# Sublayer boundaries of a conditioned trunk: three engines in written order, four weight blocks converted ahead, conditioning loads two tiles ahead

## The chip, the cores and the metric

The kernel runs on one core of one Trainium2 chip. The metric is the device time of one execution in microseconds; the kernel before was timed three times, with a median of 1191.43 us (1189.97 to 1196.67). On the core, TensorE (PE) multiplies, VectorE (DVE) and ScalarE (ACT) do the elementwise work, SyncE (SP) issues nearly all loads, and GpSimd (POOL) issues a few small ones.

## The reference, cut to what matters

Two layers, each of three sublayers: a SwiGLU feed-forward, a token mixer (HGRN2 gated recurrence in layer 0, chunked gMLP in layer 1) and another feed-forward. The input is 256 tokens of 1024 features in float32.

```python
def sublayer(x, fn, pre_g, post_g, shift, scale, gate, res_w):
    h = rms_norm(x, pre_g) * (1.0 + scale) + shift
    return x + res_w * gate * rms_norm(fn(h), post_g)

def swiglu(h, w_in, w_out):
    a, b = jnp.split(h @ w_in, 2, axis=-1)
    return (jax.nn.silu(a) * b) @ w_out
...
    cond = jax.nn.silu(c)
    for i in range(DEPTH):
        mod = (cond @ ada_w[i] + ada_b[i]).reshape(B, 3 * N_SUB, D_MODEL)[:, :, None, :]
```

`shift`, `scale` and `gate` of every sublayer are rows of `mod`, the conditioning product of a 1024-vector with a large matrix.

## The kernel before

**Split numbers.** Every float32 operand of a large product is held as two parts of TensorE's reduced float32 type: a high part (a cast) and a low part (what the cast left over). A product is three matmuls: high with high, high with low, low with high (`mm3`, lines 140 to 144; `mm3f`, 332 to 336; `chunk2`, 322 to 330, joins two of them).

**Weights.** They come in 188 blocks of 128 x 2048, in the order of use. `wblock` (112 to 125) brings one as two halves: a 512 KB load into one of four `raw` buffers, the cast by ScalarE (line 119), the subtraction by VectorE (line 120). The parts lie in tiles of the pool `whl`, twelve of them, six blocks. `next_block` converts until `ahead` blocks are in hand beyond the one it gives out. Block 33 is the first of the HGRN sublayer, 53, 86, 119 and 155 are the first of the next four.

**Conditioning.** `mod` is made of 144 tiles of 128 x 1024 (`ada`, 159 to 171): one load of 512 KB each into one of two buffers of the pool `adap`, then one multiply-and-reduce on VectorE (line 169). `pace` sets how many of them go with each block, so that those of the next sublayers are done in time. The HGRN stage asks for 18 over nine blocks (line 487). The tile `L` of its gates uses the same two buffers (line 526).

**A sublayer's end and the next one's start.** The output is accumulated in four PSUM banks `y[t][h]`, for two row tiles t of 128 tokens and two halves h of 512 features. The last two or three weight blocks of the output product are kept back, and `tail` (250 to 268) finishes one bank after another: matmuls, sum of squares on ScalarE (line 216), product with the gate (259, 263) on VectorE, root and reciprocal, residual (265). Then `nxt` (975) takes the statistics of the new x, and `prenorm` (227 to 248) scales x (233 on VectorE, 235 on ScalarE), transposes it on TensorE (239), applies scale and shift on ScalarE (243, into a float32 scratch `hf`) and makes both parts of h on VectorE (247 the high part, 248 the low part). `tail` goes through the first row tile to the end of `prenorm` and then through the second one.

The next sublayer begins with a projection of 512 columns by token tile (`proj`, 279 to 309, with `split`): four blocks, 48 matmuls a row tile. In a feed-forward (358 to 453) these are its first two units of 256 features; `post_tok` (388) applies Silu, transposes and splits them. The other units are computed transposed, by `unit2` (371), and every unit is followed by an output unit (`out_unit`, 343).

**What sets the order.** A scheduler orders the instructions of each engine from dependences, the written order as priority and its own estimate of durations; it may put work of the next sublayer into the gaps that it sees. Loads are kept in written order on SP's queue (line 56). `after` (58) ties one instruction behind another of the same engine, and `paced` (67) uses it for a matmul and `self.gate`. Each engine executes its list in order.

Of the kernel before, what the change touches and what calls it, by code (L numbers as in the profile page):

```python
# [10 lines left out]
F32 = mybir.dt.float32  # L11
# [7 lines left out]
P = 128  # L19
# [14 lines left out]
class Body:  # L34
    def __init__(self, ctx, tc, ins, out):
# [5 lines left out]
        self.whl = pool("whl", 12)  # L41
        self.act = pool("act", 1)
        self.adap = pool("adap", 2)
# [68 lines left out]
    def wblock(self, ap, n=2048):  # L112
        nc = self.nc
        hi, lo = self.wtile(), self.wtile()
        for h in range(2):
            sl = slice(h * n // 2, (h + 1) * n // 2)
            raw = self.raw.tile([P, 1024], F32, tag="raw", name="raw")[:, 0:n // 2]
            self.load(raw, ap[:, sl])
            nc.scalar.copy(hi[:, sl], raw)  # L119
            nc.vector.tensor_sub(lo[:, sl], raw, hi[:, sl])  # L120
# [4 lines left out]
        return hi, lo  # L125

    def next_block(self):

        while len(self.ready) <= self.ahead and self.blk < len(self.blocks):
            self.ready.append(self.wblock(*self.blocks[self.blk]))  # L130
            self.blk += 1
# [19 lines left out]
    def ada_setup(self):  # L151
        nc = self.nc
        self.ada_next = 0
# [5 lines left out]
    def ada(self, upto):  # L159
        nc = self.nc  # L160
        while self.ada_next < min(upto, 144):
            i = self.ada_next
            if self.ring and i % 3:
                t = self.p4.tile([P, D], F32, tag="t4", name="ada")
            else:
                t = self.adap.tile([P, D], F32, tag="ada", name="ada")
            self.load(t, self.d["ada"][i])
            junk = self.scr.tile([P, D], BF16, tag="junkv", name="junkv")
            nc.vector.tensor_tensor_reduce(junk, t, self.cond, 1.0, 0.0, ALU.mult, ALU.add,  # L169
                                           self.mod[i // 24][:, i % 24:i % 24 + 1])  # L170
# [38 lines left out]
    def rstd(self, src, second):  # L209

        nc = self.nc
        s2 = self.tiny.tile([P, 2], F32, tag="s2", name="s2")
        be = self.tiny.tile([P, 1], F32, tag="be", name="be")
        for h in range(2):
            junk = self.scr.tile([P, 512], BF16, tag="junka", name="junka")
            nc.scalar.activation(junk, src[h], AF.Square, accum_out=s2[:, h:h + 1])
            if h == 0:
                nc.vector.tensor_scalar(be, s2[:, 0:1], 1.0 / D, EPS, op0=ALU.mult, op1=ALU.add)
# [877 lines left out]
```

## Time and profile before

| what | value |
|---|---|
| median of 3 runs (lowest to highest) | 1191.43 us (1189.97 to 1196.67) |
| profiled execution: its own time | 1193.24 us |
| its span in the profile | 1191.5 us |
| granted TensorE clock over the span | 0.984 |
| VectorE busy | 888.8 us (75%) |
| ScalarE busy | 657.2 us (55%) |
| HBM read | 280.11 MB, 236 GB/s over the span |
| weight loads (raw) | 376 of 512 KB, 5.0 to 5.8 us from issue to landing by sublayer |
| conditioning loads (ada) | 144 of 512 KB, 6.5 us |

The profile is of one execution. Times in it are microseconds from the start of the span. The duration given for a matmul runs to the end of its pipeline, so that the pace of matmuls is read from one start to the next. An idle time is put down to the engine whose signal came last. In rows of groups, the numbers after the count are busy time, mean duration in ns, and the idle time before them with what ended it.

### The profile page before, as it was taken

What the parts mean: (1) busy time and instruction counts of PE and PEld (TensorE: products, weight loads), DVE (VectorE), ACT (ScalarE), POOL (GpSimd) and SP (SyncE); (2) the same over time, 40 slices, a digit from 0 to 9 for tenths busy, and PEclk for the clock granted to TensorE, in tenths of its full rate; (3) what the DMA queues carried; (4) which work ended last, traced back from release to release, by engine and by line L of the source; (5) the groups of instructions that cost most, each with busy time, mean ns of one, the idle gap of its engine ahead of it and who ended that gap; (6) DMA issues with size and microseconds to landing.
All of it is one profiled execution on the core that took longest, in us unless ns stands there. A gap on an engine that the chain in (4) does not pass through costs nothing.

```text
span 1191.5 us, 17180 instructions
## 1 busy us (share of the span) xinstructions
PE 1146.5 (96%) x6518; PEld 995.4 (84%) x6518; DVE 888.8 (75%) x1331; ACT 657.2 (55%) x1054; POOL 6.8 (1%) x16
## 2 busy tenths in 40 slices
PE   7999999997997999999999999999999999999997
PEld 6999998797895788888778888888888887888886
DVE  6997888868887887787677787657978786666652
ACT  6464446648766754456655545554754457555541
POOL 0000000000000000000000000000000000000000
PEclk9999999997999999999999999999999999999999
DMA  9899998782335777887578888537777765666640
GB/s 345 311 314 318 333 327 314 251 285 101 124 95 185 263 267 272 278 272 262 173 251 267 282 269 272 188 124 261 277 254 262 248 212 177 203 222 233 213 137 36
DMA packets 79765, 282.32 MB, mean 237 GB/s; under 512 B 9873, under 2 KB 10561, under 8 KB 79682
## 3 DMA queue, kind: packets, MB, share of 16 engines
q1 hardware_dynamic: 78626, 278.05, 68.0%
q0 software_dynamic: 1056, 3.17, 0.8%
q8 instruction: 51, 0.84, 0.3%
q14 instruction: 32, 0.26, 0.1%
HBM read 280.11 MB, written 1.07 MB: 236 GB/s over the span
## 4 chain that ended last, share of the span: by engine, by line
PE 73%; DMA 10%; DVE 8%; ACT 5%; issue 3%; SPq 0%; DVEq 0%; ACTq 0%
PE ups L328 15%; PE ups L329 8%; PE y L144 7%; PE y L142 7%; PE y L143 7%; PE ups L418 4%; DMA ada<-in_ada 4%; DMA raw<-in_wffn 4%; DVE w L120 3%; PE ups L334 3%; PE ups L336 3%; PE ups L335 3%; DMA raw<-in_whg 3%; ACT w L119 2%; PE ab L599 2%
## 5 line engine op out<-in xcount | busy, mean ns | idle before, releaser
L120 DVE TENSOR_TENSOR w<-raw,w 128x1024 fp32r<-128x1024 f32 x376 | 453.5, 1220 | 84.7 <-ACT w L119 77.5
L119 ACT CAST w<-raw 128x1024 fp32r<-128x1024 f32 x376 | 388.0, 1050 | 202.9 <-DMA raw<-in_wffn 79.4
L328 PE MATMUL ups<-h,w 128*128 128x512 f32 x864 | 303.1, 394 | 0.0
L169 DVE CUSTOM_DVE_ANT_0 junkv<-ada,cond 128x1024 bf16<-128x1024 f32 x144 | 175.8, 1221 | 92.0 <-DMA ada<-in_ada 91.5
L329 PE MATMUL ups<-h,w 128*128 128x256 f32 x864 | 242.5, 281 | 0.0
L328 PEld LDWEIGHTS ups<-h,w 128*128 128x128 f32 x864 | 162.3, 188 | 36.8
L142 PE MATMUL y<-w,t 128*128 128x512 f32 x448 | 179.4, 400 | 4.5 <-ACT t L147 4.5
L143 PE MATMUL y<-w,t 128*128 128x512 f32 x448 | 178.2, 398 | 0.0
L144 PE MATMUL y<-w,t 128*128 128x512 f32 x448 | 177.6, 397 | 0.2
L329 PEld LDWEIGHTS ups<-h,w 128*128 128x128 f32 x864 | 163.7, 190 | 0.9
L334 PE MATMUL ups<-h,w 128*128 128x256 f32 x416 | 118.3, 285 | 0.6 <-ACT w L119 0.6
L336 PE MATMUL ups<-h,w 128*128 128x256 f32 x416 | 117.8, 283 | 0.2 <-DVE w L120 0.2
L335 PE MATMUL ups<-h,w 128*128 128x256 f32 x416 | 117.6, 283 | 0.0
L142 PEld LDWEIGHTS y<-w,t 128*128 128x128 f32 x448 | 84.5, 189 | 24.1 <-ACT t L147 5.3
L144 PEld LDWEIGHTS y<-w,t 128*128 128x128 f32 x448 | 84.3, 189 | 21.0 <-DVE t L148 1.1
L143 PEld LDWEIGHTS y<-w,t 128*128 128x128 f32 x448 | 84.5, 189 | 17.9
L79 ACT ACTIVATE t<-t 128x256 f32<-128x256 f32 (+2 forms) x70 | 36.3, 523 | 97.7 <-DVE t L378 95.5
L334 PEld LDWEIGHTS ups<-h,w 128*128 128x128 f32 x416 | 79.7, 192 | 1.7 <-ACT w L119 0.8
L335 PEld LDWEIGHTS ups<-h,w 128*128 128x128 f32 x416 | 79.7, 192 | 0.8 <-issue 0.2
L336 PEld LDWEIGHTS ups<-h,w 128*128 128x128 f32 x416 | 79.7, 192 | 0.4 <-DVE w L120 0.4
L291 PE MATMUL pps<-w,h 128*128 128x512 f32 x160 | 64.4, 403 | 5.3 <-DVE h L247 5.3
L292 PE MATMUL pps<-w,h 128*128 128x512 f32 x160 | 63.8, 399 | 0.0
(199 smaller groups left out, 1435.4 us busy)
## 6 DMA issues: line engine op xcount, KB each, us to landing
raw<-in_wffn SPq DMA_DIRECT2D x264, 512.0 KB, 5.5
ada<-in_ada SPq DMA_DIRECT2D x144, 512.0 KB, 6.5
raw<-in_wgmu SPq DMA_DIRECT2D x48, 512.0 KB, 5.2
raw<-in_whg SPq DMA_DIRECT2D x40, 512.0 KB, 5.8
raw<-in_wgmv SPq DMA_DIRECT2D x24, 512.0 KB, 5.0
G<-gflat POOLq DMA_DIRECT2D x6, 512.0 KB, 5.9
t<-in_gbin SPq DMA_DIRECT2D x6, 256.0 KB, 5.2
x<-in_x SPq DMA_DIRECT2D x2, 512.0 KB, 4.0
```

What stands on the lines that cost most here:

```text
L119: nc.scalar.copy(hi[:, sl], raw)
L120: nc.vector.tensor_sub(lo[:, sl], raw, hi[:, sl])
L142: self.paced(mm(ps, l[0], r[0], start=start, stop=False))
L143: mm(ps, l[0], r[1], start=False, stop=False)
L144: mm(ps, l[1], r[0], start=False, stop=stop)
L169: nc.vector.tensor_tensor_reduce(junk, t, self.cond, 1.0, 0.0, ALU.mult, ALU.add, self.mod[i // 24][:, i % 24:i % 24 + 1])
L291: mm(res[g][t], h(0, kc), u(0, kc), start=kc == 0, stop=False)
L328: self.paced(mm(ps, u[0], self.h2[:, :, :, kc, :], start=kc == 0, stop=False))
L329: mm(ps[:, 1, :], u[1], self.h2[:, 0, :, kc, :], start=False, stop=kc == KC - 1)
L334: self.paced(mm(o, u[0], h[0], start=start, stop=False))
L335: mm(o, u[0], h[1], start=False, stop=False)
L336: mm(o, u[1], h[0], start=False, stop=stop)
```

## The change

**Order.** The new `boundary` replaces `tail` and `prenorm` between sublayers (the last `tail` stays). It opens a region in which the lists of ScalarE, VectorE and TensorE are kept as written, and `close`, in the next sublayer, ends it. The projection (`proj` now gives back a list of matmuls for each row tile), the first units of a feed-forward (`first_units`) and the first chunk of its third unit are inside.

**High parts.** `h_high` lets ScalarE write the high part of h directly from PSUM; `h_low` recomputes scale and shift on VectorE from the same PSUM bank and subtracts. One cast on VectorE goes, four small tensor_scalars come, for each half of a row tile.

**Conversions.** `cast` and `sub` do one half block; `halves(4)` and `halves(2)` stand ahead of the first and second sum of squares, so that with the one block in hand four are ready for the projection; the fifth is converted between steps of the second row tile. `hold` ties casts, subtractions and reductions written later behind the boundary's last steps. `whl` has fourteen tiles.

**Conditioning.** `ada` loads two tiles ahead of the one that it reduces, into three buffers; the reduction writes its product over its own tile; `L` uses a buffer of its own and the scratch `hf`. The paces are 23 blocks (25 before) in the first feed-forward and 22 (26) in the others, and `boundary` brings no conditioning tiles with its blocks.

**Smaller.** `out_unit` ties each of its banks behind the last matmul of the unit before; `unit2` has two more stops; the buffer for GpSimd's DMA descriptors is made 2048 bytes.

```diff
+    def cast(self):
+        if self.half is None:
+            self.half = [self.wtile(), self.wtile(), 0]
+        hi, lo, h = self.half
...
+        self.load(raw, ap[:, sl])
+        self.after(self.nc.scalar.copy(hi[:, sl], raw), self.hold[0])
...
+    def sub(self):
+        hi, lo, sl, raw, h = self.casts.pop(0)
+        self.after(self.nc.vector.tensor_sub(lo[:, sl], raw, hi[:, sl]), self.hold[1])
...
     def ada(self, upto):
...
+            for j in range(len(self.ada_tiles), min(i + (1 if self.ring else 3), 144)):
...
+                self.load(t, self.d["ada"][j])
+                self.ada_tiles.append(t)
+            t = self.ada_tiles[i]
+            self.after(nc.vector.tensor_tensor_reduce(t, t, self.cond, 1.0, 0.0, ALU.mult, ALU.add,
+                                                      self.mod[i // 24][:, i % 24:i % 24 + 1]), self.hold[1])
...
+    def inv_rms(self, st):
+        s2, be, sq, r = st
+        self.tact(sq, s2[:, 1:2], AF.Sqrt, scale=1.0 / D, bias=be)
+        self.nc.vector.reciprocal(r, sq)
+        return r
+    def residual(self, t, yg, r, st=None):
+        for h in range(2):
+            hs = slice(512 * h, 512 * h + 512)
+            self.nc.vector.scalar_tensor_tensor(self.x[t][:, hs], yg[:, hs], r, self.x[t][:, hs],
+                                                op0=ALU.mult, op1=ALU.add)
+            if st is None:
+                self.load(self.out[t][:, hs], self.x[t][:, hs])
+            else:
+                self.square(self.x[t][:, hs], st[0], h)
+                if h == 0:
+                    self.half_mean(st)
+    def h_high(self, t, h, xn, cols):
...
+        for k in range(4):
+            kc = 4 * h + k
+            last = nc.scalar.activation(self.h2[:, 0, t, kc, :], pa[:, k * P:(k + 1) * P], AF.Identity,
+                                        bias=sh[:, kc:kc + 1], scale=A[:, kc:kc + 1])
+        return pa, last
+    def h_low(self, t, h, pa, cols):
...
+            nc.vector.tensor_scalar(hf[:, ks], pa[:, ks], A[:, kc:kc + 1], sh[:, kc:kc + 1],
+                                    op0=ALU.mult, op1=ALU.add)
...
+        return nc.vector.tensor_sub(self.h2[:, 1, t, hs4, :], hf.rearrange("p (k t) -> p k t", k=4),
+                                    self.h2[:, 0, t, hs4, :])
+    def boundary(self, y, G, mm, cols, table):
...
+        self.region = self.tc.manual_schedule(engines={E.Activation, E.DVE, E.PE})
+        self.region.__enter__()
...
+        self.halves(4)
+        sy, sx, yg = self.row_stats(), self.row_stats(), ytile()
+        do(mm(0, 0))
+        sq(0, 0, sy)
+        self.half_mean(sy)
+        gated(0, 0, yg)
+        self.halves(2)
+        do(mm(0, 1))
+        sq(0, 1, sy)
+        gated(0, 1, yg)
+        r = self.inv_rms(sy)
+        self.residual(0, yg, r, sx)
+        r = self.inv_rms(sx)
+        do(mm(1, 0))
...
+        self.scaled(0, 0, xn, r)
+        sq(1, 0, sy1)
+        self.scaled(0, 1, xn, r)
+        self.half_mean(sy1)
+        gated(1, 0, yg1)
...
+        do(m[0:3])
+        pa0, _ = self.h_high(0, 0, xn, cols)
+        do(m[3:4])
+        pa1, _ = self.h_high(0, 1, xn, cols)
+        do(m[4:])
+        self.h_low(0, 0, pa0, cols)
+        self.h_low(0, 1, pa1, cols)
+        w = [[self.ready.pop(0) for _ in range(2)] for _ in range(2)]
+        self.res, go = self.proj(w)
+        sq(1, 1, sy1)
+        gated(1, 1, yg1)
+        r = self.inv_rms(sy1)
+        self.cast()
+        self.residual(1, yg1, r, sx1)
+        self.sub()
+        r = self.inv_rms(sx1)
...
+        self.halves(1)
+        p0 = go(0)
+        do(p0[0:30])
+        pa0, _ = self.h_high(1, 0, xn, cols)
+        do(p0[30:36])
+        pa1, act = self.h_high(1, 1, xn, cols)
+        do(p0[36:])
+        self.h_low(1, 0, pa0, cols)
+        dve = self.h_low(1, 1, pa1, cols)
+        self.table(table)
+        self.hold = (act, dve)
+        self.first = go(1)
...
     def out_unit(self, y, gT, wo, first):
...
+                self.gate = self.last
...
+        def first_units(pa, pb):
...
+            act(0)
+            self.halves(2)
+            do(self.first[0:30])
+            ps = turn(0)
+            split(0, ps)
+            do(self.first[30:])
+            act(1)
+            wa, wb = nb(), nb()
+            steps = unit2(wa, wb)
+            next(steps)
+            ps = turn(1)
+            split(1, ps)
+            pend.extend(gTs)
+            next(steps)
+            self.first = []
+            self.close()
+            return steps
...
-            L = self.adap.tile([P, 512], F32, tag="ada", name="L")
+            L = self.lp.tile([P, 512], F32, tag="L", name="L") if pr else self.scr.tile([P, 512], F32, tag="hf", name="L")
```

Here `act(t)` is Silu and product of a row tile, `turn` and `split` are its transposes and its split, `m[i]` is three matmuls, and `p0[i]` is one.

More of the change, by code (lines that the diff above doesn't have):

```diff
@@ L162, in ada @@
             i = self.ada_next
[L163 to L170, printed above, removed]
+            for j in range(len(self.ada_tiles), min(i + (1 if self.ring else 3), 144)):
+                if self.ring and j % 3:
+                    t = self.p4.tile([P, D], F32, tag="t4", name="ada")
+                else:
+                    t = self.adap.tile([P, D], F32, tag="ada", name="ada")
+                self.load(t, self.d["ada"][j])
[3 more added lines that the diff above has]
+                                                      self.mod[i // 24][:, i % 24:i % 24 + 1]), self.hold[1])
+            self.ada_tiles[i] = None
             self.ada_next += 1
@@ L214, in rstd, with close, tail @@
+    def close(self):
+        for op in self.first:
+            op()
+        self.region.__exit__(None, None, None)
+    def tail(self, t, y, G, mm):
+        yg = self.scr.tile([P, D], F32, tag="yg", name="yg")
+        st = self.row_stats()
         for h in range(2):
-            junk = self.scr.tile([P, 512], BF16, tag="junka", name="junka")
-            nc.scalar.activation(junk, src[h], AF.Square, accum_out=s2[:, h:h + 1])
+            for op in mm(t, h):
+                op()
+            self.square(y[t][h], st[0], h)
@@ L250, in tail @@
-    def tail(self, t, y, G, mm, nxt, last=False):
-        nc = self.nc
-        yg = self.scr.tile([P, D], F32, tag="yg", name="yg")
-        xt = self.x[t]
-        hs = [slice(0, 512), slice(512, D)]
-        mm(t, 0)
-        def second():
-            nc.vector.tensor_mul(yg[:, hs[0]], y[t][0], G[:, hs[0]])
-            mm(t, 1)
-        r = self.rstd(y[t], second)
-        nc.vector.tensor_mul(yg[:, hs[1]], y[t][1], G[:, hs[1]])
-        for h in range(2):
-            nc.vector.scalar_tensor_tensor(xt[:, hs[h]], yg[:, hs[h]], r, xt[:, hs[h]], op0=ALU.mult, op1=ALU.add)
-            if last:
-                self.load(self.out[t][:, hs[h]], xt[:, hs[h]])
-        nxt(t)
+                self.half_mean(st)
@@ L335, in mm3f @@
         mm(o, u[0], h[1], start=False, stop=False)
[L336 removed]
+        self.last = mm(o, u[1], h[0], start=False, stop=stop)
     def gtile(self):
@@ L425, in ffn @@
         else:
-            wa, wb = [[nb(), nb()] for _ in range(2)]
-            pend = post_tok(*self.proj(hT, [wa, wb], 512, split=True))
+            pend = []
+            self.pace(bg, 22)
+            steps = first_units(*self.res)
         y = self.y_banks()
-        self.pace(bg, 25 if f == 0 else 26)
+        if f == 0:
+            self.pace(bg, 23)
         for u in range(len(pend), 11):
```

241 lines of the change are left out of this document (128 added, 113 removed).

## The prediction

> **What bounds the kernel now.** I read the busy shares first, then the table by stage, then TensorE's waits stage by stage, and only then single stretches of the timeline.
>
> ```profile
> PE 1146.5 (96%) x6518; PEld 995.4 (84%) x6518; DVE 888.8 (75%) x1331; ACT 657.2 (55%) x1054; POOL 6.8 (1%) x16
> ```
>
> TensorE is busy for 1146.5 of the span's 1191.5 us. Nothing in the change takes a matmul away, so what can be won is the idle 45 us and what a lowered clock costs. The stages show where both lie: microseconds, busy time of PE, its weight loads, DVE, ACT and POOL, granted clock, DMA share, GB/s.
>
> ```profile
> 66.00:190.00 124.00, 124.00 (x853) 115.12 (x853) 102.11 (x134) 60.76 (x67) 1.21 (x2) 1.00 0.93 332
> 190.00:258.00 68.00, 64.57 (x384) 56.73 (x383) 54.80 (x89) 37.84 (x67) 0.00 (x0) 1.00 0.80 266
> 258.00:372.00 114.00, 102.24 (x669) 93.38 (x668) 94.50 (x160) 84.42 (x160) 1.07 (x2) 0.93 0.41 139
> 372.00:416.00 44.00, 39.40 (x169) 31.40 (x168) 33.93 (x53) 28.86 (x57) 0.00 (x0) 0.92 0.62 213
> 570.00:612.00 42.00, 36.54 (x157) 28.46 (x156) 31.59 (x51) 27.30 (x52) 0.00 (x0) 0.95 0.58 197
> 765.00:800.00 35.00, 34.91 (x160) 28.09 (x159) 22.50 (x38) 22.74 (x48) 0.00 (x0) 1.00 0.33 113
> ```
>
> The five boundaries between sublayers lie in 190 to 258, 372 to 416, 570 to 612, 765 to 800 and 985 to 1025; I number them 1 to 5. Inside a feed-forward sublayer (66 to 190) TensorE has no gap. Boundary 4 loses 0.1 us, the first three 3.4 to 5.5 us, and around 2 and 3 the clock is down as well. TensorE's waits (total, times, longest) in boundary 1, the HGRN stage, then boundaries 2, 3 and 5:
>
> ```profile
> PE pps L291 <- DVE h L247: 2.3, 1, 2.3
> ...
> PE npa L239 <- ACT xn L235: 1.2, 1, 1.2
> ```
> ```profile
> PE ots L663 <- DVE t L658: 4.4, 1, 4.4
> PE fps L336 <- DVE w L120: 3.1, 2, 1.7
> ```
> ```profile
> PE pps L291 <- DVE h L247: 1.8, 1, 1.8
> PE npa L239 <- DVE xn L233: 1.1, 1, 1.1
> PE tps L396 <- DVE t L393: 0.9, 1, 0.9
> PE y L142 <- ACT t L147: 0.8, 1, 0.8
> ```
> ```profile
> PE y L142 <- ACT t L147: 2.4, 1, 2.4
> PE npa L239 <- DVE xn L233: 2.1, 1, 2.1
> PE pps L291 <- DVE h L247: 0.9, 2, 0.6
> ```
> ```profile
> PE y L142 <- ACT t L147: 1.3, 1, 1.3
> PE npa L239 <- ACT xn L235: 0.5, 1, 0.5
> PE pps L291 <- DVE h L247: 0.4, 1, 0.4
> ```
>
> Boundaries 1, 2, 3 and 5 thus cost 3.5, 4.6, 5.4 and 2.2 us: 15.7 us together. Three kinds of wait recur: the transposes for the normalized row tile (npa), the projection's first matmuls for h (pps), and the work behind the first feed-forward units (tps, y).
>
> **Part 1, the written order.** Why boundary 3 waits is seen on DVE (start, duration, what, and in brackets the idle time before it):
>
> ```profile
> 571.66 1.23 DVE L169 CUSTOM_DVE_ANT_0 junkv<-ada,cond 128x1024 bf16<-128x1024 f32 x1 [5.40 <-DMA ada<-in_ada]
> ...
> 572.81 0.16 DVE L224 RECIPROCAL r<-sq 128x1 f32<-128x1 f32 x1
> ```
>
> A conditioning reduction of the next sublayer was put into the boundary; its tile had not landed, DVE stood still for 5.40 us, and the reciprocal queued behind it. The change removes this: inside a boundary no such reduction is written, and later ones are tied behind its last step. Boundary 4 shows the same chain with nothing foreign in it:
>
> ```profile
> 766.43 0.69 DVE L263 TENSOR_TENSOR yg<-y,G 128x512 f32<-128x512 f32 x1 [3.51 <-ACT junka L216]
> ...
> 770.05 0.49 DVE L233 TENSOR_SCALAR xn<-x,r 128x512 f32<-128x512 f32 x1
> ```
> ```profile
> 186.07 0.40 PE L142 MATMUL y<-w,t 128*128 128x512 f32 x1
> 186.30 0.39 PE L143 MATMUL y<-w,t 128*128 128x512 f32 x1
> ```
>
> From the second gated product to xn it takes 770.54 - 766.43 = 4.1 us. The new order adds one square, because half_mean now stands between the two residual halves on DVE, and a square goes ahead of it: 4.1 + 2 x 0.7 = 5.5 us (0.60 is the square's own row, below; 0.7 with its accumulator, an estimate). Matmuls start every 0.23 us. Where three out blocks are left (boundaries 1, 3, 4, 5) a half tile has 18 of them, 4.1 us; the first transposes come 18 + 9 matmuls after mm(0,1), so after 6.2 us: 0.7 us of slack and no wait, if the conversions written ahead are done. The second row tile has 30 matmuls of the projection (6.9 us) as cover for the same chain, one cast, one subtraction and the rest of h_low: from no wait to 1 us.
>
> What is new in front of the statistics are those conversions, four halves before the first square and two before the second:
>
> ```profile
> L120 DVE TENSOR_TENSOR w<-raw,w 128x1024 fp32r<-128x1024 f32 x376 | 453.5, 1220 | 84.7 <-ACT w L119 77.5 <-issue 4.5 <-PE y L143 0.9
> ```
>
> Boundary 3: its blocks were converted early enough in the trace of before (no wait of PE for w there), so 5.4 us of waits fall to the one below.
>
> Boundary 2 is shorter: two out blocks, 12 matmuls or 2.8 us a half. TensorE reaches the first transposes after 45 matmuls, 10.4 us; DVE has six subtractions (7.3 us), some 2 us of products and the chain of 5.5 us: 14.8 us. The wait is 4.4 us if no conversion was done before the boundary and, if all were, the 21 matmuls (4.8 us) against 5.5 us: 0.7 us. I take 2.5 in the middle, since the scheduler can still move region work ahead of what stands outside, and 1 us for the second tile. A conversion that no longer sits between the steps of finish could take up to 2 subtractions (2.4 us) off the 4.4 us wait of ots; I count nothing.
>
> Boundary 1 is the one where loads are late:
>
> ```profile
> 198.23 0.60 ACT L216 ACTIVATE junka<-y 128x512 bf16<-128x512 f32 x1 [2.63 <-PE y L144]
> ...
> 199.15 1.99 ACT L119 CAST w<-raw 128x1024 fp32r<-128x1024 f32 x2
> ...
> 207.57 1.50 ACT L243 ACTIVATE hf<-npa,shift,A 128x128 f32<-128x128 f32 x4
> ...
> 209.52 1.07 ACT L119 CAST w<-raw 128x1024 fp32r<-128x1024 f32 x1
> ```
>
> The second square ran at 198.23. The written order wants the casts of blocks 35 (199.15) and 36 (last half 209.52) ahead of it, on a queue where nothing passes. The loads come earlier: the HGRN pace (18 tiles over 9 blocks, line 487) put two conditioning loads of 0.52 MB behind each of blocks 34 and 35, and inside a boundary there are none. Four at 332 GB/s are 6.3 us, so 203.2; that is 5 us late, less 0.7 of slack: about 4. A smoother queue makes it 0; unchanged loads 11 less 0.7. I take 3 against 3.5 now: 0.5 us won.
>
> Boundary 5: the last gMLP blocks are late on DVE too; I take 1.7 us at the first transposes (bounds 0 and 4.9, four subtractions) against 0.9 now.
>
> **Part 2, the first feed-forward units.** The waits tps and y (1.7, 2.4 and 1.3 us) get the second half of the projection and a chunk of unit 2 as cover. One wait appears: the chunk's PSUM bank is that of a projection result which the second Silu must have read.
>
> ```profile
> L79 ACT ACTIVATE t<-pps 128x512 f32<-128x512 f32 x6 | 3.5, 587 | 0.0
> ```
>
> 0.59 us and the way there and back: 0.9 us, three times.
>
> **Part 3, high parts by ScalarE.** The four Identity activations stay, now writing h itself. DVE loses one cast and gains four tensor_scalars from PSUM per half:
>
> ```profile
> L247 DVE CAST h<-hf 128x512 fp32r<-128x512 f32 x20 | 8.5, 426 | 15.9 <-ACT hf L243 15.9
> ...
> L658 DVE SCALAR_TENSOR_TENSOR t<-ab,r,w 128x128 f32<-128x128 f32 x16 | 4.3, 342 | 0.1
> ```
>
> In the trace of before no such tensor_scalar stands; the nearest row, 128x128 from PSUM, is 342 ns, so 1.37 us against 0.43, at most 0.94 us more, 20 times. The high part no longer waits for DVE: its first matmuls gain 0.43 us and the handover. The low part is needed 16 matmuls (3.7 us) later, which hides the 0.94 us; without that cover it would cost 0.9 us per half.
>
> **Part 4, loads and buffers.** The HGRN stage waited 3.1 us for weights. The load queue shows why:
>
> ```profile
> 251.56 7.32 SPq L56 DMA_DIRECT2D ada<-in_ada  x3
> 258.97 17.01 SPq L56 DMA_DIRECT2D raw<-in_whg  x8
> ```
>
> Three conditioning loads waited for buffers, and the weights stood behind them for 7.3 us. The tile L no longer shares those buffers, there are three, and four to five blocks are ahead. Worth between 0 and 3.1 us plus the 8.0 us that a clock of 0.93 takes off 114 us; I take 3.1 and 2 of clock. The new queue has one weakness: load i+2 goes into the buffer of tile i-1, so SP waits for that reduction with the weights behind it. It is a rival below. Writing the reduction's product over its own tile, and the order tied to the last unit's matmul, I cost at nothing: TensorE has no gap between 66 and 190 that the scheduler filled, and DVE is at 75%.
>
> **The sum.** Boundary 1: 0.5. HGRN: 5.1. Boundary 2: 4.6 - 2.5 - 1.0 - 0.9 = 0.2, and of its clock (0.08 x 44 = 3.5 us) 1.5. Boundary 3: 5.4 - 0.9 = 4.5, and its clock, 0.05 x 42 = 2.1. Boundary 4: 0. Boundary 5: 2.2 - 1.7 - 0.9 = -0.4. Together 13.5 us. The profiled execution took 1193.24 us (1191.5 and 1.7 around it), 1.8 above the median of 1191.43; 1193.24 - 13.5 = 1179.7, and against the median 1178.
>
> The row of boundary 3 has a clock of 0.95 though no wait there exceeds 2.4 us. [...]
>
> **The rivals.** *All gaps close* (0.2): loads are early everywhere. Then 15.7 - 2.7 of waits, 5.6 of clock and 7 in the HGRN stage go: 25.6 us, 1166. For it speaks boundary 4, which already runs so; against it the casts of boundary 1.
>
> *The waits only move* (0.15): conversions hold the statistics back in 1, 2 and 5 (4, 5.4 and 5 us, more than now by 5), the HGRN weights come no earlier, and boundary 3 alone gives 6.6: about 1190. A scheduler that still slips foreign work into the region ends there too.
>
> *The load queue of the first sublayer* (0.13, slower): SP blocks on a buffer as at 251.56. From 66 to 190 it moves 124 us x 332 GB/s = 41 MB. At the 266 GB/s of the next row this takes 155 us, 31 late. The lead is some 16 us: block 35, cast at 199, is the third of a projection that starts near 209, behind the activations of 207.57, and is needed 24 matmuls (5.6 us) later, near 215. So 15 us reach TensorE, with 3 of clock, against 8 won in boundaries 2 and 3: 1201. It decides from 41 MB / (124 + 16 + 8 us) = 278 GB/s downwards. Against it: reductions whose data landed long ago free their buffers early.
>
> **How the numbers follow.** The forecast has 0.52, the rivals 0.20, 0.15 and 0.13. A measurement tells 0.5% (6 us) from no change: faster is below 1185.5, slower above 1197.4. Faster: 0.20 and the 0.52, whose own range, 1171 to 1185.5, follows from the bounds of boundaries 1, 2 and the HGRN stage: 0.72. Same 0.15, slower 0.13. The range runs from 1164, just under the rival with all gaps closed, to 1194, past the one that moves them; only the slow rival and little else lie outside.
>
> **What would show it.** Right: 570 to 612 has no wait but about 0.9 us at a unit chunk, and the clock at 1.00; no L169 line inside a boundary; pps waits for no h; the fps waits are gone. Wrong: npa waits over 3 us in boundaries 1, 2 and 5 with ACT or DVE standing before a cast or a subtraction; gaps between 66 and 190 with GB/s under 280; the fps waits as before.

## The result and the profile after

The changed kernel takes 1198.58 us (median of 20 runs, 1195.30 to 1204.04) against 1191.64 us for the kernel before on the same chip (20 runs, 1187.56 to 1196.76): a ratio of 1.0053, 95% interval 1.0039 to 1.0066. It is 6.9 us slower; the prediction was 13.5 us faster. The profiled execution took 1199.71 us with a span of 1197.9 us. First the page's line of busy times, then the table by stage with the stages of the prediction (last columns: granted clock, DMA share, GB/s).

```profile
PE 1144.4 (96%) x6518; PEld 997.4 (83%) x6518; DVE 909.9 (76%) x1391; ACT 663.3 (55%) x1054; POOL 6.8 (1%) x16
```
```profile
66.00:190.00 124.00, 123.68 (x850) 114.21 (x850) 99.36 (x134) 56.63 (x65) 1.22 (x2) 1.00 0.92 332
190.00:258.00 68.00, 59.91 (x323) 51.70 (x322) 50.63 (x84) 39.73 (x69) 0.00 (x0) 0.92 0.62 214
258.00:372.00 114.00, 101.86 (x689) 95.34 (x688) 93.92 (x161) 78.31 (x138) 1.08 (x2) 0.91 0.43 150
372.00:416.00 44.00, 34.85 (x159) 27.50 (x158) 32.36 (x62) 28.55 (x68) 0.00 (x0) 0.92 0.46 156
570.00:612.00 42.00, 40.43 (x186) 32.84 (x185) 28.50 (x52) 25.28 (x51) 0.00 (x0) 1.00 0.37 123
765.00:800.00 35.00, 33.02 (x153) 26.83 (x152) 26.65 (x52) 22.73 (x48) 0.00 (x0) 1.00 0.30 97
```

Boundary 3 (570 to 612) is near what was forecast: 40.43 us busy in place of 36.54, clock 1.00. The feed-forward stage still moves 332 GB/s with no gap worth naming. The first harm is seen in 190 to 258: 59.91 us busy in place of 64.57, 214 GB/s in place of 266, clock down to 0.92. TensorE's waits (total, times, longest), window by window, in boundary 1, the HGRN stage, and boundaries 2, 3, 4 and 5; ots belongs to the end of the HGRN stage, which now falls into the window of boundary 2:

```profile
PE npa L271 <- DVE be L242: 8.1, 1, 8.1
```
```profile
PE ab L741 <- DVE t L735: 6.6, 1, 6.6
PE ab L741 <- ACT L L679: 5.1, 1, 5.1
...
```
```profile
PE ots L805 <- DVE t L800: 5.0, 1, 5.0
PE npa L271 <- DVE xn L293: 2.4, 1, 2.4
PE npa L271 <- DVE be L242: 1.6, 1, 1.6
...
```
```profile
PE npa L271 <- DVE xn L293: 1.6, 1, 1.6
```
```profile
PE npa L271 <- DVE xn L293: 2.0, 1, 2.0
```
```profile
PE npa L271 <- DVE xn L293: 1.6, 1, 1.6
```

The waits for h, fps, tps and y are down to 0.2 us or gone. Up are the 8.1 us in boundary 1, the waits of the HGRN attention (ab: 11.7 us in the two longest, where the kernel before had 3.0 and 0.5), and one of 1.6 to 2.4 us in each of boundaries 2 to 5: the second row tile's transposes.

To see where time is lost for good, I matched the k-th matmul of TensorE in the two traces (6518 each) and took the difference of its start times. Positive: later than in the kernel before. (The lists differ in places, so that the two need not be the same product.) The columns are places, named by the time in the kernel before; the runs below the first row are the experiments.

```
         end of   HGRN   before  in the  end of  2nd     3rd   start   in    end of  end of
         1st ffn  first  attn    attn    HGRN    ffn     ffn   gMLP   gMLP   gMLP    kernel
before:   201.5   231.0  282.4   309.8   371.6  428.3   624.9  798.1  859.4  976.6   1176.2
changed    +1.0    +7.9   +0.9   +13.8   +14.1  +12.1    +3.5   +5.3  +10.7   +8.7     +6.5
a1         +0.1    +4.9   -1.3    -1.9    -1.0   -3.9   -11.6   -9.7   -3.8   -3.3     -4.8
a2         -0.6    +3.1   -3.9    +7.2    +7.3   +6.1    +0.4   +4.9  +10.8   +9.1     +8.1
a3         -0.7    +6.6   -0.5   +12.5   +12.3  +10.5    +2.0   +3.7  +11.1  +10.0     +8.3
a5         +0.5   +10.1   +7.9    +5.7   +12.5  +10.0    +2.2   +5.5  +11.7  +10.6     +8.3
b1         -0.8    +7.6   +2.8    +2.1    +3.1   +0.9    -7.2   -3.8   +3.8   +3.3     +1.9
b2         +0.4    +2.7   -3.5    -1.1    -0.6   -3.4   -11.4   -8.1   -0.8   -1.8     -2.7
b3         -0.5    +0.2   -6.8    -4.7    -4.2   -4.6    -9.1   -8.9   -8.2   -8.4     -6.2
b4         +0.3    +5.9   -0.3    +2.1    +2.8   +1.4    -6.4   -5.5   +1.4   +0.9     -1.1
c1         -1.0    +3.3   -2.6    -3.3    -2.8   -4.9   -13.4  -10.0   -9.8  -10.1    -12.4
c2         -0.4    +6.4   +0.4    +0.5    +1.0   -2.1   -10.6   -7.3   -5.6   -4.4     -6.7
c3         -0.3    +5.9   -0.2    -0.2    +0.7   -1.7   -10.2   -6.9   -5.0   -6.3     -8.5
c4         -0.8    +3.6   -2.4    +1.1    +1.4   -1.7   -10.2   -7.0   -6.6   -6.7     -9.0
d1         -0.7    +1.8   -4.4    -5.1    -4.7   -9.4   -18.1  -17.5  -17.3  -19.2    -21.6
d2         -1.0    +4.8   -0.9    -1.6    -0.7   -2.7   -10.1   -8.2   -8.0   -8.1     -9.7
d3         -0.5    +2.0   +3.3    +4.8   +12.5  +14.2   +13.8  +13.9  +21.0  +24.2    +25.2
d4         +0.2    +0.1   -6.0    -6.7    -5.7   -9.5   -17.9  -17.3  -17.1  -17.7   -20.8
```

Read the row of the changed kernel from left to right. Boundary 1 loses 6.9 us, and the HGRN features give them back (there the kernel before waited itself). The attention loses 12.9, for good. Boundary 2 wins 2.0, boundary 3 with its neighbourhood 8.6. Boundary 4 loses 1.8, gMLP 5.4. So two stages have to be explained that had no loss in the prediction: the start of the HGRN attention and that of gMLP.

The load queue of the changed kernel around boundary 1 (start, duration, engine, source, what was issued):

```profile
187.00 21.88 SPq L57 DMA_DIRECT2D raw<-in_whg  x12
208.93 24.97 SPq L57 DMA_DIRECT2D ada<-in_ada  x2
234.00 0.85 SPq L57 DMA_DIRECT2D raw<-in_whg  x2
```

And the queue's own wait between 186 and 300:

```profile
SPq L57 <- DVE mod L192: 65.5, 11, 24.2
```

Two issues of conditioning loads took 24.97 us, 24.2 of it waiting for one reduction (mod). The three buffers were full with tiles loaded ahead; their reductions are tied behind the boundary, which ends near 232; the weights of the HGRN sublayer stood behind them in the queue. In the window 208 to 232 the kernel before and the changed kernel stand so (the first row is before):

```profile
208.00:232.00 24.00, 21.16 (x96) 17.31 (x97) 20.80 (x35) 16.42 (x35) 0.00 (x0) 1.00 0.75 246
```
```profile
208.00:232.00 24.00, 18.49 (x78) 15.33 (x79) 17.16 (x39) 16.53 (x39) 0.00 (x0) 0.79 0.20 71
```

71 GB/s in place of 246. The 18 reductions that are paced through this sublayer run from 198 to 262 in the kernel before and from 232 to 302 in the changed one, eight of them after 262.

By 282.4 all this has cost 0.9 us; the 12.9 us are lost behind it. From 282 to 330 TensorE waits 11.7 us in place of 3.5, and its clock is 0.79 in place of 0.93. The longer wait, 6.6 us, ends with a product on VectorE (L735). In the changed kernel it stands behind two subtractions and the rest of a step of the gates (L685 to L690); in run a1 below, which has no such wait, the same product follows L675 at once (the changed kernel first, then a1):

```profile
306.42 0.68 DVE L675 SCALAR_TENSOR_TENSOR w<-fps,L 128x512 f32<-128x512 f32 x1
...
308.81 2.36 DVE L132 TENSOR_TENSOR w<-raw,w 128x1024 fp32r<-128x1024 f32 x2
...
313.83 0.69 DVE L735 TENSOR_TENSOR t<-t,w 128x512 f32<-128x512 f32 x1
```
```profile
300.69 0.68 DVE L675 SCALAR_TENSOR_TENSOR w<-fps,L 128x512 f32<-128x512 f32 x1
301.29 0.68 DVE L735 TENSOR_TENSOR t<-t,w 128x512 f32<-128x512 f32 x1
```

This stretch is not written in order: the scheduler made the list. Of the runs below only a2 and a3 have the changed kernel's list here, and they have the same two waits, 5.1 and 6.6 us, though a2's matmuls are 4.8 us earlier at 282.4. What leads the scheduler to this list no run shows.

### The profile page after: what moved, and what is told of

It reads as the page before. It is cut to its first block, busy times and chain, and to the rows that moved or that the text cites. A ratio compares the mean times of both kernels' runs of the same rounds, so it can differ in the third digit from the quotient of the medians.

```text
span 1197.9 us, 17119 instructions
## 1 busy us (share of the span) xinstructions
PE 1144.4 (96%) x6518; PEld 997.4 (83%) x6518; DVE 909.9 (76%) x1391; ACT 663.3 (55%) x1054; POOL 6.8 (1%) x16
## 4 chain that ended last, share of the span: by engine, by line
PE 83%; DVE 8%; DMA 4%; ACT 4%; issue 1%; SPq 0%; DVEq 0%; ACTq 0%
PE ups L437 17%; PE ups L438 9%; PE y L162 8%; PE y L163 8%; PE y L164 8%; PE pps L412 7%; PE ups L557 4%; PE ups L445 4%; PE ups L443 4%; PE ups L444 4%; DVE w L132 2%; PE ab L741 2%; DMA raw<-in_wffn 2%; ACT w L122 1%; PE vps L1003 1%
## 5 line engine op out<-in xcount | busy, mean ns | idle before, releaser
L192 DVE CUSTOM_DVE_ANT_0 ada<-ada,cond 128x1024 f32<-128x1024 f32 x144 | 173.6, 1221 | 21.7 <-DMA ada<-in_ada 21.7
L412 PE MATMUL pps<-w,h 128*128 128x512 f32 x480 | 115.1, 396 | 0.2 <-DVE h L287 0.2
L412 PEld LDWEIGHTS pps<-w,h 128*128 128x128 f32 x480 | 89.9, 190 | 19.2 <-DVE h L287 0.6
```

The source lines that it names most:

```text
L192: self.after(nc.vector.tensor_tensor_reduce(t, t, self.cond, 1.0, 0.0, ALU.mult, ALU.add, self.mod[i // 24][:, i % 24:i % 24 + 1]), self.h ...
L412: lambda g=g, i=i, j=j, kc=kc, w=w: mm(res[g][t], h2[:, i, t, kc, :], w, start=kc + i + j == 0, stop=i == 1 and kc == KC - 1)))
```

## The experiments

Theory 1: tiles loaded ahead, with reductions tied behind the boundary, stop the load queue and push the conditioning work into the attention, which loses its time by that. The rivals were the single buffers of L (theory 2) and the conversions ahead of the statistics (theory 3). Ratios are against the kernel before.

**a1: one conditioning load at a time.**

```diff
-            for j in range(len(self.ada_tiles), min(i + (1 if self.ring else 3), 144)):
+            for j in range(len(self.ada_tiles), min(i + 1, 144)):
```

> The changed kernel with one thing undone: a conditioning tile is loaded when it is reduced, not two tiles ahead (its three buffers and the order tied to the boundary stay). Theory 1 (the tiles loaded ahead are held through boundary 1, the load queue stands 24.2 us behind them, and their reductions come back in the HGRN attention): the stop of the queue at 209 goes, blocks 33 to 36 land some 4.7 us earlier (three tiles of 0.52 MB at 332 GB/s), the npa wait of 8.1 us falls to about 4, and most of the 13 us lost between 283 and 324 come back: 1184 to 1190. Theory 2 (gate_f's tile L, now in two single buffers, holds the attention up): boundary 1 gets shorter, the HGRN stage takes this back, total 1196 to 1199.

1188.28 us, 0.9954 (0.9937 to 0.9970): 1.0% faster than the changed kernel, now faster than before. The attention loses nothing (-1.3 to -1.9 in the table), though six reductions still come after 262. The wait of boundary 1 fell to 6.3 us only. The queue of a1 stops there as well, now behind the conversions that free the raw buffers. The queue's longest wait from 186 to 300 is 14.9 us; that wait and the window 208 to 232 in a1:

```profile
SPq L57 <- DVE w L132: 71.7, 23, 14.9
```
```profile
208.00:232.00 24.00, 21.20 (x91) 17.47 (x92) 17.98 (x39) 18.57 (x41) 0.00 (x0) 0.86 0.36 128
```

**a5: the tie undone for the reductions.**

```diff
-            self.after(nc.vector.tensor_tensor_reduce(...), self.hold[1])
+            nc.vector.tensor_tensor_reduce(...)
```

> The changed kernel, but the conditioning reductions are no longer tied behind the last step of the boundary (casts and subtractions still are). Theory 1: the reductions of tiles 46 to 48 run before or inside boundary 1, where VectorE waits, the load queue does not stop, at most two reductions stand in the attention's start: 8 to 13 us won in the HGRN stage and 2 to 4 in gMLP, 1184 to 1190; one foreign reduction may cost a boundary 1.2 us. Theory 2: the HGRN stage keeps its 5.1 us wait for L, total 1195 to 1199.

1196.59 us, 1.0025 (1.0004 to 1.0047): only 0.3% better than the changed kernel, and its runs spread from 1192.97 to 1203.43 (profiled span: 1199.8). The stop of 24 us is gone (the longest is now 17.4 us, behind the conversions), but the first reductions moved to 187 and 190 and the next only to 216; the attention's start costs nothing any more (+7.9 to +5.7), while 6.8 us go in its second half, where two reductions now stand (at 333 and 343; the first is shown) that the kernel before runs at 381 and 395:

```profile
333.47 1.22 DVE L192 CUSTOM_DVE_ANT_0 ada<-ada,cond 128x1024 f32<-128x1024 f32 x1
```

That these two cause the later loss was not tried.

**a2: two of the six halves behind the first gated product of the second row tile, in every boundary** (some expectations call it the second gated product).

```diff
-        self.halves(2)
         do(mm(0, 1))
...
         gated(1, 0, yg1)
+        self.halves(2)
```

> The changed kernel with the two halves that stand ahead of the second square written behind the second gated product, in all five boundaries. Theory 3 (casts ahead of the statistics cost boundary 1 its 8.1 us): the wait falls to 4 to 5.5 us there, and in the others by up to 1 us; if nothing downstream takes it back, 1192 to 1195. Theory 1: what boundary 1 gains is taken back before 283, where the matmuls wait for weights of a stopped load queue: 1196 to 1199.

1202.34 us, 1.0079 (1.0053 to 1.0104). In boundary 1 the wait fell from 8.1 to 4.1 us, and against the changed kernel the lead lasts: 4.8 us at 231 (1.6 of them from the start of the execution), 6.8 at the end of HGRN. Then boundaries 3 and 4, which wait 2.4 and 2.8 us in place of 1.6 and 2.0, and the stages around them spend it (3.1 left at 625, 0.4 at 798). So theory 3 is right about the wait, and theory 1 is not borne out where it says that the stage before 283 takes the gain back; but moving these halves in all boundaries spends in 3 and 4 what it wins in 1.

**a3: two buffers for L** (to make room, `bc` in gMLP has one buffer, not two).

```diff
-        self.lp = pool("lp", 1)
+        self.lp = pool("lp", 2)
...
-            L = self.lp.tile(...) if pr else self.scr.tile([P, 512], F32, tag="hf", name="L")
+            L = self.lp.tile([P, 512], F32, tag="L", name="L")
```

> The changed kernel with two buffers for the tile L of gate_f (in the changed kernel each pair has one single buffer, the first shared with the scratch of h_low); to make room the gMLP tile bc has one buffer in place of two. Theory 2: the 5.1 us wait of the attention for L goes, and with it 5 to 8 us of the HGRN stage: 1190 to 1194. Theory 1: L was late since VectorE and ScalarE were behind with held work; the HGRN stage stays within 1.5 us, total 1196 to 1200.

1200.44 us, 1.0055 (1.0039 to 1.0070), and the same two waits of the HGRN stage to the tenth:

```profile
PE ab L741 <- DVE t L735: 6.6, 1, 6.6
PE ab L741 <- ACT L L679: 5.1, 1, 5.1
```

Theory 2 has fallen. The name in this wait (L, 5.1 us) was that of the last link, not the cause.

**b1: both undone** (the edits of a1 and a5).

> The changed kernel with both undone: a conditioning tile is loaded when it is reduced, and its reduction is not tied behind the boundary. Theory 1a (the load queue standing behind tied reductions did all the harm; with one tile at a time the tie itself costs nothing): as the run with the loads alone undone, 1188.3, within 4 us. Theory 1b (the tie alone also pushes reductions into the attention): 3 to 6 us faster than that run, 1182 to 1185. Rival: untied reductions get back into boundaries as before the change (1.2 us each, or the wait of 5.4 us for a tile that has not landed): 2 to 6 us slower than it.

1193.87 us, 1.0015 (1.0001 to 1.0028), by the ratios 0.6% slower than a1. The tie is worth having when one tile is loaded at a time; without it two reductions go back into boundary 1, and VectorE stands in front of the first, with h_low behind both:

```profile
212.20 1.23 DVE L192 CUSTOM_DVE_ANT_0 ada<-ada,cond 128x1024 f32<-128x1024 f32 x1 [1.81 <-DMA ada<-in_ada]
```

**b3: part 4 alone, in the kernel before** (three buffers, loads two ahead, the product over its own tile, L in buffers of its own; nothing tied).

> The kernel before with part 4 alone: three conditioning buffers, loads two tiles ahead, the product written over the tile, L in buffers of its own; boundaries, conversions and first units as before. Theory 1 (loads ahead do harm only through reductions that are tied behind a written boundary): reductions run where their tiles have landed, the queue has no stop over 10 us at boundary 1, time within 4 us of the kernel before. Rival (loads ahead of the weights cost the weights their turn by themselves): boundary 1 or the HGRN stage loses 4.7 us or more (three tiles of 0.52 MB at 332 GB/s), 1196 or slower.

1185.61 us, 0.9940 (0.9926 to 0.9955), better than either side expected. 302 GB/s between 208 and 232, more than the 246 of the kernel before:

```profile
208.00:232.00 24.00, 21.77 (x95) 16.91 (x96) 21.69 (x39) 16.52 (x32) 0.00 (x0) 1.00 0.86 302
```

So loading ahead wins in the kernel before, where the reductions may run at once, and loses in the changed one, where they may not.

**b2: a1, and block 36's halves late in boundary 1 alone** (`if self.nbound == 1` around the edit of a2).

> Loads one at a time as in the first run, and in boundary 1 alone the two halves of block 36 stand behind the second gated product. Theory 3a (boundary 1 is paid in full once the load queue runs): its npa wait falls from 6.3 us to 1 to 3 and the time by 3 to 5 us, 1183 to 1185. Theory 3b (the HGRN feature stage that follows is bound by blocks being converted on VectorE or loaded, so that an earlier start waits there): the offset is the same again at 283, 1187 to 1189.

1187.49 us, 0.9964 (0.9951 to 0.9977): no gain over a1. The matmuls are 2.2 us earlier than in a1 at 231, still 2.2 at 282, and 0.8 later in the attention. Theory 3b has the outcome right and the place wrong: not the feature stage takes the gain back but the attention's start behind it.

**b4: a1, and another order for the second row tile on VectorE** (gated product and residual ahead of the second half of h_low, half_mean behind both residual halves).

> Loads one at a time as in the first run, and for the second row tile another order on VectorE: the gated product and the residual ahead of the second half of h_low, both residual halves ahead of half_mean, the subtraction behind the second scaled half. Theory 4 (the second row tile's chain is late by 1.6 to 2.6 us in boundaries 2 to 5 since the 4.1 us of h_low stand ahead of its gated product): these waits fall under 0.5 us, up to 0.5 us each comes up at the low-part matmuls, 5 to 7 us faster than the first run, 1181 to 1183. Rival (what comes next on VectorE or in the loads takes it back): within 2 us of the first run, 1186 to 1190.

1187.01 us, 0.9964 (0.9948 to 0.9980), as a1. The waits for xn are gone and the low parts wait in their place:

```profile
PE pps L417 <- DVE h L287: 6.4, 5, 2.4
```

**c1: a1, and gMLP paced as in the kernel before.** The changed kernel, a1, a5, b1 and b4 lose 5.4 to 7.6 us between 798 and 859; b3 loses 0.7. `pace` counts the blocks that bring conditioning tiles; four of gMLP's are now converted inside the boundary, where none counts.

```diff
-        self.pace(bg, 30, 6)
+        self.pace(bg, 26, 2)
```

> Loads one at a time as in the first run, and in gMLP the conditioning tiles paced over 26 blocks after 2 in place of 30 after 6, since four of the blocks that the kernel before counted are now converted inside the boundary, where none is counted. Theory 5 (the three gate tiles come in one burst at 813, after the last v blocks, where the kernel before had them between the blocks; so gps waits for the gate and the next conversions behind it): the offset gained from 820 to 870 falls from 6 us to under 2, 4 to 6 us faster than the first run, 1182 to 1184. Rival (gMLP loses them to the place of the converted blocks, or to VectorE's order): within 1.5 us of the first run.

1181.68 us, 0.9909 (0.9896 to 0.9922): 0.45% better than a1, as theory 5 said. The queue in the kernel before, in the changed one and in c1:

```profile
811.38 0.42 SPq L56 DMA_DIRECT2D ada<-in_ada  x1
812.14 2.09 SPq L56 DMA_DIRECT2D raw<-in_wgmv  x2
```
```profile
820.31 7.26 SPq L57 DMA_DIRECT2D raw<-in_wgmv  x4
827.62 0.90 SPq L57 DMA_DIRECT2D ada<-in_ada  x2
```
```profile
801.34 0.42 SPq L57 DMA_DIRECT2D ada<-in_ada  x1
802.10 2.09 SPq L57 DMA_DIRECT2D raw<-in_wgmv  x2
```

Before and in c1 the tiles that the gate needs lie between the weights; in the changed kernel they come in a pair behind the last of them. TensorE's waits from 800 to 875 are 4.1 us there, from the gate's transposes (gps, at 838) on, against 0.8 in the kernel before and 0.9 in c1.

**d3: the late pace alone, in the kernel before.** The opposite test.

```diff
-        self.pace(bg, 9)
+        self.pace(bg, 9, 4)
...
-        self.pace(bg, 30, 6)
+        self.pace(bg, 30, 10)
```

> The kernel before with one number changed in two places: conditioning tiles of HGRN paced from four blocks later on, and those of gMLP from ten blocks on in place of six, as the changed kernel has it since the blocks converted inside a boundary do not count. Theory 5/6 (the late pace alone costs the HGRN and gMLP stages): offsets of 2 to 6 us arise in 258 to 320 and 4 to 7 us in 820 to 870: 1196 to 1203. Rival (the pace matters only with the written order): within 3 us of the kernel before in each stage, 1190 to 1195.

1216.51 us, 1.0184 (1.0147 to 1.0221): 23 us slower, the direction of theory 5 and 6 and far more than their size. The two paces were not tried one by one. Of the 25.2 us in its trace 10.5 come up between 231 and 372, where three reductions now stand in the attention (at 309, 316 and 322; the first is shown), and 10.3 in gMLP.

```profile
309.44 1.21 DVE L169 CUSTOM_DVE_ANT_0 junkv<-ada,cond 128x1024 bf16<-128x1024 f32 x1
```

**c2: loads two ahead and the tie kept, but all loaded tiles reduced at the start of a boundary.**

```diff
-            for j in range(len(self.ada_tiles), min(i + (1 if self.ring else 3), 144)):
+            for j in range(len(self.ada_tiles), min(i + (1 if self.ring else self.lead), 144)):
...
+        self.lead = 1
+        self.ada(len(self.ada_tiles))
+        self.lead = 3
         self.halves(4)
```

> The changed kernel with its loads two tiles ahead and its tie, but every tile already loaded is reduced at the start of each boundary, ahead of the first conversions, and none is loaded until the boundary's weights are. Theory 1 (a loaded tile that must wait for the boundary is what stops the queue): no stop over 10 us at 209, HGRN start as with one load at a time or better; 10 to 15 us faster than the changed kernel, 1184 to 1189. Rival (the two loads ahead cost by themselves under the written order; three reductions, 3.9 us, hold the statistics up in five boundaries): under 6 us faster, 1193 or more.

1187.59 us, 0.9959 (0.9946 to 0.9973), 11 us faster than the changed kernel. Loading ahead does no harm when the buffers are empty at the entry, as theory 1 said. But its account of the way there does not hold: the npa wait of boundary 1 is still 8.1 us, the queue still stops for 14.4 us (behind the conversions; no stop over 10 was expected), and eight reductions come after 262 as in the changed kernel, yet the attention loses 0.1 us. VectorE's list there has a1's order, with the product right behind the gate step. In gMLP c2 loses 1.7 us with the late pace kept.

**c3 and c4: c2 with the pace of c1, and the same with boundary 1 as in b2.**

> The kernel that reduces the loaded tiles at the start of each boundary, and gMLP paced over 26 blocks after 2. If theories 1 and 5 add up: 4 to 6 us faster than without the pace, 1179 to 1184, with only the wait in boundary 1, the second row tiles and the attention's own waits left. Rival: with loads ahead the gate tiles are early anyhow and the pace changes under 1.5 us.

> The same with both, and in boundary 1 alone the two halves of block 36 behind the second gated product. Theory 3a: now that neither queue nor VectorE is late in the HGRN stage, boundary 1's 3 to 5 us come out at the end: 1176 to 1180. Theory 3b (the attention's start is bound by its own chain on ScalarE and VectorE, as when loads go one at a time): within 1.5 us of the kernel without it.

c3: 1185.50 us, 0.9946 (0.9932 to 0.9959); c4: 1183.47 us, 0.9924 (0.9912 to 0.9937). The pace is worth 2.1 us here, less than 4 to 6, and moving the halves of block 36 another 2.0; in the traces c4 is no earlier than c3 at 310, so that its gain is not pinned to boundary 1.

**d2: c1, and three conditioning tiles loaded and reduced inside boundary 1.**

> Loads one at a time and gMLP paced as above (1181.7), but in boundary 1 three conditioning tiles are loaded behind the weights of the boundary and reduced inside it (one behind the second gated product, two behind the last conversion), and three more are loaded there. Theory 6 (what the HGRN stage still loses is conditioning work that boundary 1 no longer carries: 128 GB/s in 208 to 232 against 246 before, and 12 reductions by 262 against 18): more GB/s in 208 to 232, two or three reductions fewer after 262, 2 to 4 us faster, 1178 to 1180. Rival (the attention's start is bound by its own chain anyhow): the matmuls are earlier at 283 and no earlier at 310; within 1.5 us.

1184.30 us, 0.9915 (0.9884 to 0.9946), no gain over c1. Reductions ran at 211, 225 and 226, but six still came after 262, as in c1, and the wait of boundary 1 rose from 5.8 to 7.3 us. The edit did not take reductions out of the attention, as theory 6 needs, so that it does not settle theory 6.

**d1: c1, and half_mean behind both residual halves** (in both row tiles; the subtraction of the second one's chain behind its scaled halves).

```diff
             else:
                 self.square(self.x[t][:, hs], st[0], h)
-                if h == 0:
-                    self.half_mean(st)
+        if st is not None:
+            self.half_mean(st)
...
```

> Loads one at a time and gMLP paced over 26 blocks after 2 (1181.7), and half_mean behind both residual halves in place of between them, the subtraction in the second row tile's chain behind its scaled halves; h_low stays where it is. Theory 4 (the square that half_mean puts into the chain, 0.94 us from the square's start to the next, is what the first tile of boundary 2 and the second tiles of boundaries 2 to 5 wait for): these five waits of 1.6 to 2.6 us each fall by 0.8 to 0.9, no pps wait for h appears as it did when h_low moved: 3 to 4.5 us faster, 1177 to 1179. Rival (what PE gains is waited for a few us later, at the low parts or the next conversions): within 1.5 us, 1180.5 to 1183.

1176.28 us, 0.9855 (0.9817 to 0.9893): 5.4 us under c1 (0.5% by the ratios), more than the 3 to 4.5 expected. VectorE at the second row tile of boundary 3, first in a1, which has the order of the change there, then in d1:

```profile
573.45 1.37 DVE L284 TENSOR_SCALAR hf<-npa,A,shift 128x128 f32<-128x128 f32 x4 [1.82 <-ACT h L274]
...
577.67 0.68 DVE L310 TENSOR_TENSOR yg<-y,G 128x512 f32<-128x512 f32 x1
...
580.00 0.15 DVE L242 TENSOR_SCALAR be<-s 128x1 f32<-128x1 f32 x1 [0.79 <-ACT junka L235]
580.07 0.74 DVE L255 SCALAR_TENSOR_TENSOR x<-yg,r,x 128x512 f32<-128x512 f32 x1
...
582.26 0.49 DVE L293 TENSOR_SCALAR xn<-x,r 128x512 f32<-128x512 f32 x1
```
```profile
572.18 0.68 DVE L310 TENSOR_TENSOR yg<-y,G 128x512 f32<-128x512 f32 x1
...
572.97 1.42 DVE L255 SCALAR_TENSOR_TENSOR x<-yg,r,x 128x512 f32<-128x512 f32 x2
574.51 0.16 DVE L242 TENSOR_SCALAR be<-s 128x1 f32<-128x1 f32 x1
...
575.86 0.49 DVE L293 TENSOR_SCALAR xn<-x,r 128x512 f32<-128x512 f32 x1
```

From gated product to xn it takes 582.75 - 577.67 = 5.1 us in a1 and 576.35 - 572.18 = 4.2 in d1. The wait of TensorE there falls from 1.6 to this:

```profile
PE npa L271 <- DVE xn L293: 0.7, 1, 0.7
```

**d4: d1, and boundary 1 as in b2.**

> As the first of these (half_mean behind both residual halves), and in boundary 1 the two halves of block 36 behind the second gated product. If boundary 1's wait counts now: 2 to 4 us faster than the first of these, 1174 to 1177. Theory 3b (the attention's start takes it back, as before): within 1 us of it.

1172.17 us (1170.02 to 1174.59), 0.9815 (0.9781 to 0.9849), the best kernel of the study, 1.9% faster than before. Whether the last edit adds to d1 is not settled: the medians are 4 us apart, but the two intervals overlap, the profiled spans are 1170.6 and 1169.9 us, and in the traces d4's lead over d1, 1.6 us in the attention, is down to 0.1 at 428.

## Why the prediction was wrong

**The load queue.** Part 4 saw the weakness ("load i+2 goes into the buffer of tile i-1, so SP waits for that reduction with the weights behind it"), and the rival of the first sublayer looked for it in the wrong place. Between 66 and 190 the queue keeps its 332 GB/s, as the argument against it said: there no reduction is tied, and the queue's longest wait for one is 6.6 us. Ahead of a boundary they may not run, because the same change ties them. The tie is in the text ("later ones are tied behind its last step") as a gain of boundary 3 and nowhere as a cost. The rival's 1201 lies near the measured 1198.58 by luck: it rests on 15 us lost between 66 and 190, and nothing is lost there. The other two rivals did not happen either. This is the step that failed first: two parts of the change were costed one by one, and each is a gain by itself (b3, part 4 alone, 0.9940; a1, the tied boundary without loads ahead, 0.9954), while together they are 1.0053. Undoing the tie of the reductions in place of the loads ahead gave only 1.0025 (a5).

**Part 4** put 5.1 us to the credit of the HGRN stage; this is the term of the sum that failed most. Measured: 12.9 us lost in the attention. Of these 8.2 are longer waits of TensorE (11.7 against 3.5 between 282 and 330), and the clock, 0.79 there against 0.93, can account for the rest (0.14 x 48 = 6.7 us at most, an estimate). The stop of the queue, which theory 1 blamed, had cost 0.9 us by then, and a1 and c2, with six and eight late reductions and stops of 14.9 and 14.4 us, lose nothing there. The waits go with the list that the scheduler gave VectorE in the attention. That this list comes with loads ahead and full buffers at a tied boundary is what the runs show; why it does stays open. b3, part 4 without the tie, is 3.7 us better at the end of HGRN than at its start and 6.7 us in all, so the size was about right for a queue that runs.

**The pace.** The prediction used the conditioning tiles that boundary 1 no longer loads as a gain ("the loads come earlier", 6.3 us) and never asked where they go. They come four blocks later, in HGRN and in gMLP; the change adapted the paces of the feed-forwards and left these two. gMLP had no term in the sum, and lost 5.4 us; in c1 it loses 0.2 where a1 loses 5.9, and the time is 0.45% shorter. d3 shows both late paces together costing 23 us in the kernel before; that of HGRN was not put back in the changed kernel.

**Boundary 1** was taken as 3 us, from 0 to 10.3; it is 8.1. The second square ran at 207.17 and not at 203.2, with the cast of block 36 just ahead of it. Without loads ahead (a1) that cast starts at 203.52, as worked out; but 203.2 was the start of the cast, the square comes behind it at 204.48, and the wait is 6.3 us. So the loads ahead added 1.8 us, and the term was too small by itself: the square's 6.3 us of lateness against 198.23 came through whole, with no slack to set against it.

```profile
206.22 1.05 ACT L122 CAST w<-raw 128x1024 fp32r<-128x1024 f32 x1 [0.52 <-DMA raw<-in_whg]
207.17 0.59 ACT L235 ACTIVATE junka<-y 128x512 bf16<-128x512 f32 x1
```

That wait alone was not the loss: the HGRN features took it back. Of shortening it b2 kept nothing at the end and a2 spent it in boundaries 3 and 4.

**Boundaries 2 to 5.** Boundary 3 was right (forecast 6.6 us won, measured 8.6 with what lies around it, clock 1.00). The first tile of boundary 2 waits 1.6 us where 2.5 was taken, boundary 5 in all 1.6 where 2.6 was. The term for the second row tile ("from no wait to 1 us") failed in each: 2.4, 1.6, 2.0 and 1.6 us. The chain itself was nearly right, 5.1 us against 5.5; its start was not. The gated product stands behind both halves of h_low on VectorE (at 577.67 in a1, behind 4.2 us of them: 573.45 to 577.67), which the text had as "the rest of h_low". d1 takes the square out of the chain and 0.8 to 1.3 us off each wait. (In the rival whose waits only move, the parts for boundaries 1, 2 and 5 are 4.1 us more than the waits of now, not 5; nothing hangs on it.)

**Parts 2 and 3.** The 0.9 us of the chunk's PSUM bank (the Silu's measured 0.59 us, and 0.3 us for the way there and back, the author's estimate) did not appear. The price of h_low came out at its upper bound, 1.37 us for four, and the wait of the projection for it is 0.2 us, as hidden as predicted, though the same 4 us are what the second row tile stood behind.

```profile
L284 DVE TENSOR_SCALAR hf<-npa,A,shift 128x128 f32<-128x128 f32 x80 | 27.3, 406 | 11.9 <-ACT h L274 10.9
```

27.3 us for 80 are 0.34 each in sequence. With one load at a time and gMLP's pace put back, c1 takes 1181.68 us. That d1 and d4, at 1176 and 1172 us, go past the forecast of 1178 does not confirm its sum: they hold an order of the second row tile that the change did not have.

## What to carry to other kernels

When an order is fixed by hand, list for every buffer filled before the fixed stretch who empties it and whether that may happen inside: a prefetch whose consumer is tied behind the stretch stopped the queue here for 24.2 us, with all that stood behind it. Then look at the list that the scheduler makes of the free stretch behind the fixed one, since it too can change. When work is moved out of a counted loop, look at everything that the loop's count paced. And cost the parts of a change together as well as one by one: here two gains made a loss.

## What the runs showed of the hardware

The same wait of TensorE in boundary 2 (2.4 us, the second row tile's) was followed by half a clock in the changed kernel and not in a1. Windows of the changed kernel, then of a1, each with the wait in its first row (clock 1.00 in both) and what came behind it in the second:

```profile
406.00:410.00 4.00, 1.59 (x9) 1.06 (x8) 2.60 (x5) 2.80 (x7) 0.00 (x0) 1.00 0.13 36
410.00:413.40 3.40, 3.40 (x12) 2.67 (x11) 3.04 (x6) 2.23 (x8) 0.00 (x0) 0.53 0.64 176
```
```profile
391.00:395.00 4.00, 1.57 (x9) 1.02 (x8) 2.64 (x6) 2.73 (x7) 0.00 (x0) 1.00 0.06 8
395.00:399.00 4.00, 4.00 (x22) 3.35 (x21) 3.08 (x6) 3.90 (x10) 0.00 (x0) 1.00 0.64 174
```

So behind a wait of the same length one kernel had a clock of 0.53 for 3.4 us, some 1.6 us more (an estimate from these rows, 0.47 x 3.4), and the other had 1.00. Why the clock fell behind the one and not behind the other was not shown. Part of d1's surplus over its expected 4.5 us may be such a difference: in 372 to 416 the clock is 0.96 in c1 and 1.00 in d1. That was not tried by itself.
